# Three more ring slots from one large tile: storing the norm's input as four tiles, and tying the PSUM additions of a down projection behind a weight split

## The chip, the cores and the metric

The kernel runs on one core of a Trainium2 chip. The metric is the device time of one execution in microseconds. Before the change it is 2233.83 us, the median of three runs (2231.4, 2234.19 and 2233.83).

## What is computed

One layer of a streaming encoder for 256 tokens of width 2048, all in float32: a half-step SwiGLU FFN, two parallel token mixers (latent attention and RWKV7), cross-attention into 256 memory tokens, and a second half-step FFN. Only the two FFNs are touched by what follows, the down projection above all:

```
def rmsnorm(x, g): return x * rsqrt(mean(x * x, -1) + 1e-6) * g
def swiglu(h, w_gate, w_up, w_down):
    return (silu(h @ w_gate) * (h @ w_up)) @ w_down       # 256x2048 -> 256x5504 -> 256x2048

x = x + 0.5 * rmsnorm(swiglu(rmsnorm(x, n_ffn1_pre), ...), n_ffn1_post)
x = x + rmsnorm(mixers(rmsnorm(x, n_mix_pre)), n_mix_post)
x = x + rmsnorm(cross_attention(rmsnorm(x, n_x_pre), mem), n_x_post)
x = x + 0.5 * rmsnorm(swiglu(rmsnorm(x, n_ffn2_pre), ...), n_ffn2_post)
```

## The kernel before

**A weight tile's way.** Every weight is read once. A tile of 128 x 1024 float32 (512 KB) is loaded by SP's DMA queue into one of the four buffers `wraw` (L335, in the wide part L525). ScalarE casts it to the matmul's 32-bit type (`whi`, L343, L510) and VectorE subtracts the cast from the raw tile (`wlo`, L344, L511); the text calls the two a split, and `last_cast` and `last_split` name the latest ones. Both go to a slot of a ring: `RING` = 3 slots of `whi` and `wlo`. TensorE then does three products for each (activation high with weight high, high with low, low with high: L438 to L440, in the wide part L518 to L520), each with 512 columns.

**Order on the engines.** Each engine takes its instructions in the order of its own list, and so does SP, whose list is mostly loads: an instruction that waits holds all behind it. A scheduler makes these lists from the program and from priorities (`ahead(n)` moves a step n places forward); `after(a, b)` ties instruction a behind b. In the down projections TensorE's order is as written.

**The down projection.** 5504 rows are 43 blocks of 128, the 2048 columns two halves (b = 0 and 1) of 1024, each of them two chunks of 512 (c = 0, 1 and c = 2, 3). For a half the order is:

1. `lin_wide` (L496): the first 30 blocks over all 1024 columns. 16 blocks are single tiles of 12 matmuls. The other 14 go in 7 pairs, for which a scheme of Strassen's kind saves an eighth: a pair loads two tiles, splits half of one and the whole other, then VectorE makes four sums in place in the raw tiles (L543 to L546) and both are split again, for 21 matmuls. So a half has 30 loads, 44 splits and 339 matmuls. These splits go to a ring of six slots: the three of `whi` and `wlo`, then three in `room`, a 32 KB-per-partition tile that takes the place of `hT` (the norm's output, the FFN's input). Each half starts at slot 0.
2. `narrow`: early tiles e0 to e2 of the odd chunk (blocks 30 to 35 of c + 1, 128 x 1024 each: two blocks of 512 columns), in the ring of three.
3. `fix_wide` (L558): the pairs left four shared partial sums p1, p5, p7, p6 in PSUM. One ScalarE copy (L566) and eight VectorE additions and subtractions (L567 to L574) add them to the half's own four banks. A `wraw` buffer, `part`, holds the intermediate values. They have the priority `ahead(3 * self.lead)`.
4. `narrow`: n0 to n6, the last 13 blocks of the even chunk (n6 is one block, 128 x 512), after which the chunk is done: ScalarE squares and sums it (L617) and VectorE scales it by the gain (L758).
5. `narrow`: f0 to f3, the last 7 blocks of the odd chunk. In the first FFN's b = 1, f0 and f1 are split into slots of a `Passage`, which sit in the next norm's `hT`.

Then the residual X (2 MB) is loaded by four SP loads of 512 KB (L877), tied behind the latest split; the first FFN's X comes from the input x, the second's from `xsp`, where the running sum was stored. In the first FFN the next projection's weights (`w_in`) follow on SP, in the second X stands ahead of the very last weight tile.

Of the kernel before, what the change touches and what calls it, by code (L numbers as in the profile page):

```python
# [108 lines left out]

class Passage:  # L110
# [3 lines left out]
    def __init__(self, L, gain, spill=None, keep=None):  # L114
        self.L, self.gain, self.spill = L, gain, spill if keep is None else keep
        self.wide = spill is not None
        self.h = L.hpool.tile([P, KD, 2, T], F32R, tag="hT", name="hT", bufs=1)
        flat = self.h.rearrange("p k a t -> p (k a t)")
        at = lambda i: flat[:, KD * T + i * WT : KD * T + (i + 1) * WT]
# [84 lines left out]
class Layer:  # L204
# [291 lines left out]
    def lin_wide(self, w, b, mh, ml, sums, ring, banks):  # L496
# [25 lines left out]
        def load():  # L522
            raw = self.wraw.tile([P, WT], F32, tag="wraw", name="wraw")
# [7 lines left out]
        for item in _wide_order():  # L531
# [24 lines left out]
            product(own[1][0], at(k1, 1), e4)  # L556

    def fix_wide(self, banks, part):  # L558


        nc = self.nc
        own, (p1, p5, p7, p6) = banks
        u, v = part[:, :512], part[:, 512:]
        add, sub = nc.vector.tensor_add, nc.vector.tensor_sub
        with self.ahead(3 * self.lead):
            nc.scalar.copy(out=u, in_=p1)  # L566
            add(own[0][0], own[0][0], u)  # L567
            add(u, p6, u)
            sub(v, p5, u)
            add(u, p7, u)  # L570
            add(own[1][0], own[1][0], u)
            add(own[0][1], own[0][1], v)
            sub(v, v, p7)
            add(own[1][1], own[1][1], v)  # L574
# [71 lines left out]
    def pre_norm(self, gain, update):  # L646

        nc = self.nc
        h = self.hpool.tile([P, KD, 2, T], F32R, tag="hT", name="hT", bufs=1)
# [19 lines left out]
    def pre_norm_input(self, srcT, gain, pool, squares, order=False):  # L669
# [4 lines left out]
        h = pool.tile([P, KD, 2, T], F32R, tag="hT", name="hT", bufs=1)  # L674
# [95 lines left out]
    def ffn(self, normed, wg, wu, wd, post, residual, *after):  # L770
# [3 lines left out]
        with self.tc.tile_pool(name="hid", bufs=1) as hid:  # L774
# [32 lines left out]
            for c0 in range(0, DFF, 256):  # L807
# [38 lines left out]
            room = self.hpool.tile([P, KD * 2 * T], F32R, tag="hT", name="room", bufs=1)  # L846
            slots = [(x[:, a : a + WT], z[:, d : d + WT]) for x, z, d0 in (
                (self.whi, self.wlo, 0), (room, room, RING * SLOT)) for a in range(0, RING * SLOT, SLOT) for d in (a + d0,)]
            banks = {}

            def narrow(c, ks, ev, *args):
                base = c // 2 * KF * P * WT + (WIDE * WT + c % 2 * (KF - WIDE) * 512) * P
                self.lin_tok(
                    wd, KF, 0, 512, mh, ml, ev, *args, 0, [banks[c // 2][0][t][c % 2] for t in range(NT)],
                    (ks, lambda k: base + (k - WIDE) * P * 512))

            def lin(c, ev, passage):
# [9 lines left out]
                with self.tc.manual_schedule(engines={mybir.EngineType.PE}):  # L867
                    self.lin_wide(wd, b, mh, ml, lambda n: [(x[:, 0], x[:, 1]) for x in (sums(n)[:, i] for i in range(3))],
# [1036 lines left out]
```

## Time and profile before

The page is of one profiled execution; `PE` is TensorE's matmuls, `DVE` VectorE, `ACT` ScalarE, `SP` the queue that issues the loads.

| | us |
|---|---|
| median of three runs | 2233.83 |
| the profiled execution | 2234.2 |
| its span | 2232.4 |
| mean granted TensorE clock | 0.994 of full |
| VectorE busy | 1621.1 (73%) |
| ScalarE busy | 1190.6 (53%) |
| DMA | 453.51 MB, mean 203 GB/s |

The first FFN's down projection runs from 461 to 686 us, the second's from 1999 to 2219 us; the rest of the program isn't touched in TensorE's order. In a row of the timeline the bracket at the end is the idle time ahead of the instruction and what ended it.

### The profile page before, as it was taken

What the parts mean: (1) busy time and instruction counts of PE and PEld (TensorE: products, weight loads), DVE (VectorE), ACT (ScalarE), POOL (GpSimd) and SP (SyncE); (2) the same over time, 40 slices, a digit from 0 to 9 for tenths busy, and PEclk for the clock granted to TensorE, in tenths of its full rate; (3) what the DMA queues carried; (4) which work ended last, traced back from release to release, by engine and by line L of the source; (5) the groups of instructions that cost most, each with busy time, mean ns of one, the idle gap of its engine ahead of it and who ended that gap; (6) DMA issues with size and microseconds to landing.
All of it is one profiled execution on the core that took longest, in us unless ns stands there. A gap on an engine that the chain in (4) does not pass through costs nothing.

```text
span 2232.4 us, 35351 instructions
## 1 busy us (share of the span) xinstructions
PE 2176.8 (98%) x13580; PEld 1929.9 (86%) x13580; DVE 1621.1 (73%) x2402; ACT 1190.6 (53%) x1794; POOL 106.2 (5%) x177
## 2 busy tenths in 40 slices
PE   9999999999999999999999999999999999999997
PEld 8999999987878889988777889988999999988786
DVE  7777666687787667777777766557777766678685
ACT  7555555554545655664444556446555555555453
POOL 0000000000000100101342000000000000000000
PEclk9999999999999999999999999999999999999998
DMA  7666666655657664555867765556666666666655
GB/s 250 203 200 203 202 199 202 202 191 188 206 188 264 204 219 146 185 177 180 254 197 242 271 210 189 175 174 218 198 200 202 201 200 201 203 197 203 204 199 178
DMA packets 132361, 453.51 MB, mean 203 GB/s; under 512 B 16352, under 2 KB 17888, under 8 KB 131936
## 3 DMA queue, kind: packets, MB, share of 16 engines
q1 hardware_dynamic: 124560, 434.03, 59.7%
q0 software_dynamic: 6768, 16.79, 2.5%
q8 instruction: 106, 1.74, 0.3%
q14 instruction: 63, 0.52, 0.1%
q10 hardware_dynamic: 864, 0.44, 0.1%
HBM read 438.61 MB, written 12.59 MB: 202 GB/s over the span
## 4 chain that ended last, share of the span: by engine, by line
PE 68%; DVE 11%; DMA 9%; issue 7%; ACT 4%; POOL 1%; SPq 0%; ACTq 0%; DVEq 0%; POOLq 0%
PE mm L399 30%; PE mm L403 15%; DMA wraw<-in_w_ffn_down 7%; PE mm L439 6%; PE mm L438 6%; PE mm L440 6%; DVE wlo L344 3%; DVE room L511 3%; ACT whi L343 2%; DVE wlo L511 1%; ACT room L510 1%; DVE wraw L545 1%; PE mm L519 1%; PE mm L520 1%; DMA squares<-in_xT 1%
## 5 line engine op out<-in xcount | busy, mean ns | idle before, releaser
L344 DVE TENSOR_TENSOR wlo<-wraw,whi 128x1024 fp32r<-128x1024 f32 (+3 forms) x672 | 807.1, 1203 | 433.1 <-ACT whi L343 424.6
L399 PE MATMUL mm<-hT,whi 128*128 128x512 f32 x3280 | 1077.0, 383 | 1.7 <-ACT whi L343 1.1
L343 ACT CAST whi<-wraw 128x1024 fp32r<-128x1024 f32 (+3 forms) x672 | 691.5, 1030 | 594.1 <-PE mm L440 240.6
L403 PE MATMUL mm<-hT,wlo 128*128 128x256 f32 x3280 | 879.4, 273 | 0.8 <-DVE wlo L344 0.8
L399 PEld LDWEIGHTS mm<-hT,whi 128*128 128x128 f32 x3280 | 613.2, 189 | 82.9 <-ACT whi L343 2.6
L403 PEld LDWEIGHTS mm<-hT,wlo 128*128 128x128 f32 x3280 | 628.9, 192 | 7.4 <-DVE wlo L344 1.9
L439 PE MATMUL mm<-wlo,hT 128*128 128x512 f32 (+2 forms) x512 | 180.3, 352 | 4.1 <-DVE wlo L344 3.8
L438 PE MATMUL mm<-whi,hT 128*128 128x512 f32 (+2 forms) x512 | 182.5, 357 | 0.9 <-DVE gt L1564 0.7
L440 PE MATMUL mm<-whi,hT 128*128 128x512 f32 (+2 forms) x512 | 178.3, 349 | 0.1
L411 ACT COPY half<-mm 128x256 f32<-128x256 f32 x206 | 75.8, 369 | 116.2 <-PE mm L399 116.2
L510 ACT CAST whi<-wraw 128x1024 fp32r<-128x1024 f32 x92 | 94.2, 1046 | 66.0 <-DVE wraw L546 38.5
L511 DVE TENSOR_TENSOR wlo<-wraw,whi 128x1024 fp32r<-128x1024 f32 x92 | 110.4, 1222 | 16.9 <-ACT whi L510 16.1
L510 ACT CAST room<-wraw 128x1024 fp32r<-128x1024 f32 (+1 forms) x84 | 74.0, 903 | 84.9 <-DMA wraw<-in_w_ffn_down 71.9
L412 DVE TENSOR_TENSOR half<-half,mm 128x256 f32<-128x256 f32 x206 | 86.1, 418 | 39.9 <-ACT half L411 39.8
L439 PEld LDWEIGHTS mm<-wlo,hT 128*128 128x128 f32 x512 | 97.1, 190 | 19.1 <-DVE wlo L344 10.5
L518 PE MATMUL mm<-whi,mh 128*128 128x512 f32 x284 | 109.1, 384 | 4.5 <-ACT whi L510 4.5
L519 PE MATMUL mm<-wlo,mh 128*128 128x512 f32 x284 | 109.3, 385 | 1.6 <-DVE wlo L511 1.6
L520 PE MATMUL mm<-whi,ml 128*128 128x512 f32 x284 | 108.9, 383 | 0.0
L438 PEld LDWEIGHTS mm<-whi,hT 128*128 128x128 f32 x512 | 97.1, 190 | 12.6 <-DVE gt L1564 1.1
L440 PEld LDWEIGHTS mm<-whi,hT 128*128 128x128 f32 x512 | 97.1, 190 | 9.7 <-DVE hT L626 1.0
L511 DVE TENSOR_TENSOR room<-wraw,room 128x1024 fp32r<-128x1024 f32 (+1 forms) x84 | 86.1, 1045 | 17.1 <-ACT room L510 16.5
L590 POOL TENSOR_TENSOR rstd<-rstd,mhalf 128x1 f32<-128x1 f32 x22 | 15.4, 705 | 1724.3 <-DVE rstd L588 1724.3
(361 smaller groups left out, 2752.3 us busy)
## 6 DMA issues: line engine op xcount, KB each, us to landing
wraw<-in_w_ffn_up SPq DMA_DIRECT2D x171, 512.0 KB, 4.2
wraw<-in_w_ffn_gate SPq DMA_DIRECT2D x170, 512.0 KB, 4.2
wraw<-in_w_ffn_down SPq DMA_DIRECT2D x168, 512.0 KB, 4.4
wraw<-in_w_in SPq DMA_DIRECT2D x124, 512.0 KB, 4.0
wraw<-in_w_o SPq DMA_DIRECT2D x32, 512.0 KB, 4.2
wraw<-in_w_ckv SPq DMA_DIRECT2D x32, 512.0 KB, 3.6
wraw<-in_w_oa SPq DMA_DIRECT2D x16, 512.0 KB, 3.5
wraw<-in_w_ob SPq DMA_DIRECT2D x16, 512.0 KB, 4.6
```

The source lines that it names most:

```text
L343: cast = self.last_cast = nc.scalar.copy(out=hi[:, e], in_=raw[:, e])
L344: self.last_split = nc.vector.tensor_sub(out=lo[:, e], in0=raw[:, e], in1=hi[:, e].bitcast(F32))
L399: both = lambda: nc.tensor.matmul(ps[j], hi[:, s], self.woven(x[:, k]), start=(k == 0), stop=(k == nk - 1))
L403: nc.tensor.matmul(ps[j][:, 0, :], lo[:, s], self.woven(x[:, k, 0]), start=False, stop=False)
L438: nc.tensor.matmul(ps[t], part(xh, t, k), hi, start=(k == first and not begun), stop=False, **more)
L439: nc.tensor.matmul(ps[t], part(xh, t, k), lo, start=False, stop=False, **more)
L440: self.last_mm = nc.tensor.matmul(ps[t], part(xl, t, k), hi, start=False, stop=(k == last), **more)
L510: self.last_cast = nc.scalar.copy(out=hi, in_=raw)
L511: self.last_split = nc.vector.tensor_sub(out=lo, in0=raw, in1=hi.bitcast(F32))
L518: nc.tensor.matmul(bank, xh, hi, start=start, stop=False)
L519: nc.tensor.matmul(bank, xh, lo, start=False, stop=False)
L520: nc.tensor.matmul(bank, xl, hi, start=False, stop=stop)
```

## The change

- `hT`, the `Passage`'s copy of it, and `mT` are each four tiles of 8 KB per partition instead of one of 32 KB (`Quarters` passes indices on to them). In a down projection three of the four are `room` slots, each with high and low part, and the fourth, `raws`, is two more raw buffers: of six loads in `lin_wide` four go to `wraw` and two to `raws`.
- The wide ring begins at the narrow ring's next slot (`self.turn`) instead of slot 0, and `self.turn` moves on by the wide part's 44 splits.
- `fix_wide` loses its priority; its copy is tied behind the cast, and its first addition behind the split, of the latest tile written ahead of it (e2).
- In b = 1, X's loads no longer follow all tiles: `narrow` steps issue them at blocks 30, 33, 36 and 39 of c = 2, each tied behind the latest split. A step of `lin_tok_steps` comes once for each of the two token blocks, so each X load is issued twice.

```diff
+def quarters(pool, name="hT"):
+    return Quarters([pool.tile([P, 4, 2, T], F32R, tag="hT", name=name, bufs=4) for _ in range(4)])
...
-        self.h = L.hpool.tile([P, KD, 2, T], F32R, tag="hT", name="hT", bufs=1)
+        self.h = quarters(L.hpool)
...
         def load():
-            raw = self.wraw.tile([P, WT], F32, tag="wraw", name="wraw")
+            i = self.wide_at % 6
+            raw = raws[:, i - 4] if i > 3 else self.wraw.tile([P, WT], F32, tag="wraw", name="wraw")
...
+        self.cuts = turn[0]
...
-        with self.ahead(3 * self.lead):
-            nc.scalar.copy(out=u, in_=p1)
-            add(own[0][0], own[0][0], u)
...
+        self.after(nc.scalar.copy(out=u, in_=p1), self.last_cast)
+        self.after(add(own[0][0], own[0][0], u), self.last_split)
...
-            room = self.hpool.tile([P, KD * 2 * T], F32R, tag="hT", name="room", bufs=1)
...
+            room = [self.hpool.tile([P, 2, WT], F32R, tag="hT", name="room", bufs=4) for _ in range(RING)]
+            raws = self.hpool.tile([P, 2, WT], F32, tag="hT", name="raws", bufs=4)
...
+            def refill(k):
+                i = (k - WIDE) // 3
+                if "X" in fresh and i < 4:
+                    t, s = i // 2, slice(i % 2 * 1024, (i % 2 + 1) * 1024)
+                    self.after(nc.sync.dma_start(
+                        out=fresh["X"][:, t, s], in_=residual[t * P : (t + 1) * P, s]), self.last_split)
...
+                for k in self.lin_tok_steps(
...
+                    if c == 2 and k % 3 == WIDE % 3:
+                        refill(k)
...
+                    order = slots[self.turn :] + slots[: self.turn]
                     self.lin_wide(wd, b, mh, ml, lambda n: [(x[:, 0], x[:, 1]) for x in (sums(n)[:, i] for i in range(3))],
-                                  slots, banks[b])
+                                  order + more, raws, banks[b])
+                    self.turn = (self.turn + self.cuts % (2 * RING)) % RING if self.cuts % (2 * RING) < RING else self.turn
                     narrow(c + 1, range(WIDE, EARLY, 2), None, 0, None)
                     self.fix_wide(banks[b], self.wraw.tile([P, WT], F32, tag="wraw", name="part"))
+                    if b:
+                        self.X = fresh["X"] = self.hpool.tile([P, NT, D], F32, tag="big", bufs=1, name="X")
                     narrow(c, range(WIDE, KF, 2), ev, 0, None)
-                if b:
-                    self.X = self.hpool.tile([P, NT, D], F32, tag="big", bufs=1, name="X")
...
```

TensorE's and GpSimd's orders stay as they were. SP, in the first FFN's b = 1, before: the tail of the wide loads, the first row of which is L525, then the narrow tiles (L335), X (L877) and the next projection.

```order
L525 DMA wraw<-in_w_ffn_down 128x1024 x21
L335 DMA wraw<-in_w_ffn_down 128x1024 x9
L335 DMA wraw<-in_w_ffn_down 128x512
L335 DMA wraw<-in_w_ffn_down 128x1024 x3
L335 DMA wraw<-in_w_ffn_down 128x512
L877 DMA X<-in_x 128x1024 x4
L335 DMA wraw<-in_w_in 128x1024 x4
```

SP at the same place after: L357 is the narrow tiles' load (the first six of them e0 to n2), L879 the X load.

```order
L357 DMA wraw<-in_w_ffn_down 128x1024 x6
L879 DMA X<-in_x 128x1024 x2
L357 DMA wraw<-in_w_ffn_down 128x1024
L879 DMA X<-in_x 128x1024 x2
L357 DMA wraw<-in_w_ffn_down 128x1024
L879 DMA X<-in_x 128x1024
L357 DMA wraw<-in_w_ffn_down 128x1024
L357 DMA wraw<-in_w_ffn_down 128x512
L879 DMA X<-in_x 128x1024 x2
L357 DMA wraw<-in_w_ffn_down 128x1024 x2
L879 DMA X<-in_x 128x1024
L357 DMA wraw<-in_w_ffn_down 128x1024
```

Eight X loads now stand among the narrow tiles n2 to f2, where four stood behind f3. The first two X loads and the fifth are first loads, tied behind the splits of n0, n1 and n3; the third, fourth and sixth write the same bytes again, each behind the landing of the load that it repeats; the seventh is the fourth quarter (behind n4's split) and the eighth its repeat. The second FFN has the same pattern, with `xsp` for `in_x`.

VectorE at `fix_wide` of b = 1 in the first FFN, before: L344 is the split of a narrow tile, the first of them e0's, and L567 to L574 are the additions.

```order
L344 TENSOR_TENSOR wlo<-wraw,whi 128x1024
L567 TENSOR_TENSOR mm<-mm,part 128x512
L344 TENSOR_TENSOR wlo<-wraw,whi 128x1024
L568 TENSOR_TENSOR part<-mm,part 128x512
L569 TENSOR_TENSOR part<-mm,part 128x512
L344 TENSOR_TENSOR wlo<-wraw,whi 128x1024
L570 TENSOR_TENSOR part<-mm,part 128x512
L571 TENSOR_TENSOR mm<-mm,part 128x512
L344 TENSOR_TENSOR wlo<-wraw,whi 128x1024 x2
L572 TENSOR_TENSOR mm<-mm,part 128x512
```

After: L366 is the narrow split, and L590 to L597 are the additions.

```order
L366 TENSOR_TENSOR wlo<-wraw,whi 128x1024 x3
L590 TENSOR_TENSOR mm<-mm,part 128x512
L591 TENSOR_TENSOR part<-mm,part 128x512
L592 TENSOR_TENSOR part<-mm,part 128x512
L593 TENSOR_TENSOR part<-mm,part 128x512
L594 TENSOR_TENSOR mm<-mm,part 128x512
L366 TENSOR_TENSOR wlo<-wraw,whi 128x1024 x2
L595 TENSOR_TENSOR mm<-mm,part 128x512
L596 TENSOR_TENSOR part<-part,mm 128x512
L366 TENSOR_TENSOR wlo<-wraw,whi 128x1024
L597 TENSOR_TENSOR mm<-mm,part 128x512
```

The splits of e0 to e2 moved ahead of all additions; the next two (n0, n1) stand behind five of them.

VectorE a little later, at the end of n6 in the second FFN's b = 1, before: the first row holds splits n2 to n5, then come n6's (512 columns), f0's and f1's; L758 is the chunk's scaling by the gain.

```order
L344 TENSOR_TENSOR wlo<-wraw,whi 128x1024 x4
L344 TENSOR_TENSOR wlo<-wraw,whi 128x512
L344 TENSOR_TENSOR wlo<-wraw,whi 128x1024 x2
L758 TENSOR_TENSOR y<-mm,g 128x512
L344 TENSOR_TENSOR wlo<-wraw,whi 128x1024
L758 TENSOR_TENSOR y<-mm,g 128x512
```

After: n3 to n5, n6, the scaling (L781) of the first token block, two small steps of its sum of squares, and only then f0.

```order
L366 TENSOR_TENSOR wlo<-wraw,whi 128x1024 x3
L366 TENSOR_TENSOR wlo<-wraw,whi 128x512
L781 TENSOR_TENSOR y<-mm,g 128x512
L608 TENSOR_REDUCE tot<-ss 128x1
L609 TENSOR_SCALAR tot<-tot 128x1
L366 TENSOR_TENSOR wlo<-wraw,whi 128x1024
L781 TENSOR_TENSOR y<-mm,g 128x512
```

The splits of f0 and f1 moved behind the scaling. On ScalarE the casts moved in the same way: f0's now stands behind the first square (L640, L617 before), where f0's and f1's stood ahead of it. In the first FFN it is the same in b = 1, where f0 to f3 stood ahead.

More of the change, by code (lines that the diff above doesn't have):

```diff
@@ L845, in ffn @@
                 self.lin_ch(wu, KD, c0, n, h, ev_up)
[L846 to L848 removed]
+            room = [self.hpool.tile([P, 2, WT], F32R, tag="hT", name="room", bufs=4) for _ in range(RING)]
+            raws = self.hpool.tile([P, 2, WT], F32, tag="hT", name="raws", bufs=4)
+            slots = [(self.whi[:, a : a + WT], self.wlo[:, a : a + WT]) for a in range(0, RING * SLOT, SLOT)]
+            more = [(x[:, 0], x[:, 1]) for x in room]
+            fresh = {}
+            def refill(k):
[4 more added lines that the diff above has]
+                        out=fresh["X"][:, t, s], in_=residual[t * P : (t + 1) * P, s]), self.last_split)
             banks = {}
```

48 lines of the change are left out of this document (28 added, 20 removed).

## The prediction

> **What bounds the kernel now.** I read the page's busy times first, then TensorE's waits, then a table of stretches over the two down projections, then timelines around the stalls.
>
> ```profile
> PE 2176.8 (98%) x13580; PEld 1929.9 (86%) x13580; DVE 1621.1 (73%) x2402; ACT 1190.6 (53%) x1794; POOL 106.2 (5%) x177
> PE mm L439 <- DVE wlo L344: 11.2, 13, 2.3
> PE mm L519 <- DVE wlo L511: 9.1, 18, 1.0
> PE mm L518 <- ACT whi L510: 5.0, 4, 3.4
> ```
>
> TensorE is the bound: busy for 2176.8 of 2232.4 us, and its order doesn't change. So the change can only remove, or add, waits of TensorE. L518 and L519 are the wide part, L439 mostly the narrow tiles. The stretches (columns: length, then busy time and count of PE, PEld, DVE, ACT, POOL, then clock, DMA share and GB/s; for each half the wide part, then the narrow tiles):
>
> ```profile
> 461.20:541.10 79.90, 76.42 (x339) 64.87 (x339) 68.03 (x76) 42.25 (x47) 0.00 (x0) 0.98 0.56 189
> 541.10:575.00 33.90, 31.56 (x137) 27.11 (x138) 19.27 (x22) 11.65 (x16) 0.00 (x0) 0.95 0.56 180
> 575.00:657.00 82.00, 78.91 (x358) 66.73 (x357) 67.57 (x74) 43.60 (x50) 0.00 (x0) 1.00 0.63 205
> 657.00:694.00 37.00, 34.35 (x151) 29.05 (x149) 23.87 (x31) 15.72 (x21) 0.55 (x1) 0.95 0.71 234
> 1987.00:2064.00 77.00, 73.97 (x337) 62.66 (x336) 67.04 (x76) 42.67 (x47) 0.00 (x0) 1.00 0.61 200
> 2064.00:2098.70 34.70, 34.70 (x162) 30.38 (x162) 21.60 (x24) 14.52 (x18) 0.00 (x0) 1.00 0.67 212
> 2098.70:2180.00 81.30, 76.20 (x341) 64.97 (x340) 68.55 (x75) 42.95 (x50) 0.00 (x0) 0.98 0.57 194
> 2180.00:2221.00 41.00, 36.78 (x155) 30.66 (x155) 21.41 (x28) 13.94 (x19) 0.45 (x1) 0.92 0.55 179
> ```
>
> A matmul that isn't held up starts 0.216 us after the one before (the first two rows below: 539.47 and 539.68). So a stretch loses its length less 0.216 times its count: 79.90 - 339 x 0.216 = 6.7 us, then 4.3, 4.7, 4.4, 4.2, -0.3, 7.6 and 7.5. That is 39 us, and with 1.2 us just ahead of the first stretch (below) **40 us** are there to be won. TensorE at the first half's `fix_wide`, at two starts of a wide part, and VectorE beside the first:
>
> ```profile
> 539.47 0.38 PE L519 MATMUL mm<-wlo,mh 128*128 128x512 f32 x1
> 539.68 0.38 PE L520 MATMUL mm<-whi,ml 128*128 128x512 f32 x1
> 541.19 0.48 PE L438 MATMUL mm<-whi,mh 128*128 128x512 f32 x1 [1.13 <-ACT whi L343]
> 543.92 0.48 PE L439 MATMUL mm<-wlo,mh 128*128 128x512 f32 x1 [2.24 <-DVE wlo L344]
> 544.53 0.63 PE L438 MATMUL mm<-whi,mh 128*128 128x512 f32 x1
> 544.96 0.63 PE L439 MATMUL mm<-wlo,mh 128*128 128x512 f32 x1
> ...
> 461.24 0.48 PE L518 MATMUL mm<-whi,mh 128*128 128x512 f32 x1 [1.18 <-ACT whi L510]
> 462.50 0.80 PE L519 MATMUL mm<-wlo,mh 128*128 128x512 f32 x1 [0.78 <-DVE wlo L511]
> ...
> 2102.51 0.48 PE L518 MATMUL mm<-whi,mh 128*128 128x512 f32 x1 [3.35 <-ACT whi L510]
> ```
>
> ```profile
> 537.75 1.23 DVE L344 TENSOR_TENSOR wlo<-wraw,whi 128x1024 fp32r<-128x1024 f32 x1 [1.68 <-ACT whi L343]
> 538.89 0.69 DVE L567 TENSOR_TENSOR mm<-mm,part 128x512 f32<-128x512 f32 x1
> 541.32 0.68 DVE L568 TENSOR_TENSOR part<-mm,part 128x512 f32<-128x512 f32 x1
> 542.65 1.22 DVE L344 TENSOR_TENSOR wlo<-wraw,whi 128x1024 fp32r<-128x1024 f32 x1
> ```
>
> After a stall matmuls start 0.43 us apart (544.53, 544.96) at half rate, for about nine: 9 x 0.21 = 1.9 us on top of the wait.
>
> **The change part by part.**
>
> *Ring order.* A wide part starts with slot 0 whichever slot the narrow tiles used last, so its first cast can wait for a slot that TensorE has only just left: the two starts above cost 1.18 + 0.78 + 1.9 = 3.9 us and 3.35 + 1.9 = 5.3 us, 9.2 together. With the oldest slot first the cast comes two tiles earlier, 24 matmuls or 5.2 us, more than either wait. I take 8.2 and leave 1.
>
> *Six raw buffers.* SP's wide loads wait for VectorE to give a raw buffer back, and VectorE and ScalarE in turn for landings (views of the waits in the first FFN):
>
> ```profile
> SPq L525 <- DVE wraw L545: 53.0, 9, 6.8
> DVE wraw L544 <- DMA wraw<-in_w_ffn_down: 6.9, 10, 1.0
> ACT room L510 <- DMA wraw<-in_w_ffn_down: 38.4, 26, 3.3
> ```
>
> The steady loss of the wide parts is what the starts leave: 6.7 + 1.2 - 3.9 = 4.0, then 4.7, 4.2 and 7.6 - 5.3 = 2.3: 15 us. VectorE is busy for some 68 us of a half whose 339 matmuls need 73.2, so it can keep up, with 5 us to spare, if it needn't wait for landings. Two more buffers let SP issue two loads earlier; a half's 30 loads take 73.2 us, so two are 4.9 us, more than the longest of these waits (3.3). With so thin a margin I take 11 and leave 4; ends: 0 (VectorE is the bound) and 15.
>
> *`fix_wide`'s tie.* Before, additions of 0.69 us stand among the splits of e0 to e2, and these splits release TensorE (row 543.92). The narrow stretches lose 4.3, 4.4, -0.3 and 7.5 us, of which about 1 is the last tile (below). With all three splits ahead, e0 to e2 give TensorE 36 x 0.216 = 7.8 us; five additions take 3.5 us and n0's split 1.2, so they lie beside that work, if e2's split ends by 3 us into it. I take 14.5 and leave 0.5. If that cover is gone, 2 us per half come back.
>
> *X's place.* Before, X stood ahead of the last tile of the second FFN; about 1 us of waiting ahead of that tile goes (counted above). Removed in all: 8.2 + 11 + 14.5 + 1 = **35 us**.
>
> *What X adds.* Every X load is issued twice, the repeat waits for the first's landing, and SP holds the weight tiles behind it. Landings of narrow weight tiles (541 to 564 us), of X in the first FFN, and in the second:
>
> ```profile
> DMA to landing us min/median/max: 3.4/4.2/5.4
> ...
> DMA to landing us min/median/max: 6.4/7.6/8.7
> ...
> DMA to landing us min/median/max: 7.3/8.6/9.7
> ```
>
> Call the landing time L. The second X load goes out at n1's split, its repeat and then n4's load at L after it, and n4 is there after 2L. A narrow tile is 12 x 0.216 = 2.59 us of TensorE. n1's cast waits for the end of e1, three tiles before in the ring; cast (1.05) and split (1.23) end 2.3 us later. n4's cast can start at the end of n1, 7.8 us after that of e1, and may come 2.9 us later still before TensorE waits. So n4 costs 2L - 8.4: nothing at 4.2, 1.6 at 5, 6.8 at 7.6. The same reckoning for f2 (the last repeat goes ahead of it, at n4's split) gives 2L - 13: nothing up to 6.5. Between n2 and f2 some 4 MB of weights and 4 MB of X pass in 26 us, 310 GB/s where the narrow stretch had 234 at a share of 0.71. So L is above 4.2; the 7.6 and 8.6 were of four loads issued at once. I take 5, nearest to the unhurried row.
>
> The Trainium skill ("DMA: Bandwidth & Descriptors", Anatomy of one DMA) fits a transfer as 2.0 us plus bytes over 436 GB/s, for GpSimd's path. By it 512 KB land in an estimated 3.2 us, n4 costs nothing and the sum is 3.2 us less; the row has 4.2 here and no such landing under 3.4.
>
> *f0 behind the square.* In b = 1 the cast of f0 now waits for the chunk's first square, thus for nearly the end of n6. The second FFN's end, ScalarE then VectorE:
>
> ```profile
> 2211.27 0.59 ACT L617 ACTIVATE junk<-mm 128x512 f32<-128x512 f32 x1
> 2211.85 1.03 ACT L343 CAST whi<-wraw 128x1024 fp32r<-128x1024 f32 x1
> 2217.28 0.62 ACT L343 CAST whi<-wraw 128x512 fp32r<-128x512 f32 x1 [3.80 <-DMA wraw<-in_w_ffn_down]
> ...
> 2212.54 0.68 DVE L758 TENSOR_TENSOR y<-mm,g 128x512 f32<-128x512 f32 x1
> 2213.14 1.22 DVE L344 TENSOR_TENSOR wlo<-wraw,whi 128x1024 fp32r<-128x1024 f32 x1
> ```
>
> The square begins at the end of the first token block's products, three matmuls (0.65 us) before n6 ends. Square, cast and split, 0.59 + 1.03 + 1.22 = 2.84, less 0.65 and the one matmul that needs no split (0.22), leave 2.0; with handovers 2.4. It is split in two like the pair of waits at 461.24 (1.18 and 0.78), after which matmuls ran at half rate: 1.9 more. The ends are 2.0 and 4.3.
>
> The Trainium skill ("TensorE: Matmul & The Clock Gate", What's actually happening) has TensorE go to half rate after an idle window of some 3.4 us. By it the new stalls stay at full rate and the sum is 2 x 1.9 = 3.8 us less. Here the rows at 461 speak against it, with two waits of 1.96 us in all.
>
> Added: 1.6 + 2.4 + 1.9 = 5.9 per FFN, **12 us** in both. The profiled execution took 2234.2, its span 2232.4, and lies 0.4 above the median: 2234.2 - 35 + 12 = **2211 us**.
>
> **The rivals.**
>
> *All is hidden.* L stays at 4.2, the stalls of f0 stay at full rate, the wide parts lose nothing: 2234.2 - 40 + 2 x 2.4 = 2199. For it: the unhurried row. Against: 310 GB/s. Chance 0.14.
>
> *VectorE is the bound of the wide parts.* The raw buffers then bring nothing: 2211 + 11 = 2222. For it: 68 of 73.2 us busy, in which every handover counts. Against: the rows that end in a landing. Chance 0.14.
>
> *The repeats hold SP's queue.* At the 9.2 us to which the X rows reach, n4 costs 10.0, f2 5.4, f0 with half rate 4.3 and a second half-rate stretch 1.9: 21.6 per FFN, 43 in both, and 2234.2 - 35 + 43 = 2242, slower. It decides from 2L - 8.4 + 2L - 13 + 6.2 = 17.5 per FFN, which is L = 8.2. For it: X's own rows of 7.6 and 8.6. Against: these were four at once with 2 MB of weights behind. Chance 0.06; L within 0.2 of 8.2 leaves the time as it was.
>
> *The change doesn't reach TensorE*, because what SP waits for in the wide part isn't buffers but VectorE's own pace, and the new stalls eat the rest. With L near 7.6 and the raw buffers idle, 35 - 11 = 24 us go and 2 x (6.8 + 2.2 + 6.2) = 30 come: 2240, slower too; with L at 6.5 it is 2 x (4.6 + 6.2) = 22 and about 2232. Chance 0.05 for no change, 0.02 for slower.
>
> **How the numbers follow.** Some 0.2% (4.5 us) is what a measurement tells from no change. My case, 2205 to 2219, has 0.59; hidden 0.14 and VectorE-bound 0.14 are faster too: 0.87. No change has 0.05, slower 0.08. The range reaches from the hidden case, 2198, to L = 7 in my case (5.6 + 1 + 6.2 = 12.8 per FFN, 2234.2 - 35 + 26 = 2225); above it lie the 0.13 of the last two rivals, and some 0.05 of tails lie outside on either side.
>
> **What would show it.** In the profile after: at the four starts of the wide parts no wait of L518 above 0.5 us; VectorE's waits on landings in the wide parts gone, TensorE at 73 to 74.5 us for 339 matmuls; no wait between e0 and n1; in each b = 1 a wait for f0's cast and split of 2 to 2.5 us, matmuls 0.43 us apart after it, and n4 late by 1 to 2. I am wrong if X lands in 7 us or more, if the wide parts still take over 76 us, or if SP's repeats cost nothing.

## The result and the profile after

The changed kernel takes 2213.14 us (median of four runs, 2210.27 to 2216.57), the kernel before 2233.84 beside it: a ratio of 0.991, 95% interval 0.9893 to 0.9927, thus 20.7 us faster. The forecast was 2211, range 2198 to 2225. The profiled execution of the changed kernel is the slowest of the four (2216.57, span 2214.7), so its profile shows 17.6 us less than the profile before.

The first row is TensorE's of the page; then come the eight stretches, cut this time at the first matmul of each wide part and of each e0 (columns as before):

```profile
PE 2170.6 (98%) x13580; PEld 1929.0 (87%) x13580; DVE 1618.7 (73%) x2402; ACT 1189.7 (54%) x1794; POOL 106.0 (5%) x177
```

```profile
460.77:537.82 77.05, 75.39 (x341) 65.17 (x339) 68.53 (x77) 43.70 (x48) 0.00 (x0) 0.98 0.63 221
537.82:571.49 33.67, 33.67 (x158) 29.48 (x156) 20.82 (x24) 15.25 (x19) 0.00 (x0) 1.00 0.67 212
571.49:644.66 73.17, 73.17 (x341) 64.07 (x340) 67.14 (x74) 41.70 (x47) 0.00 (x0) 1.00 0.62 205
644.66:690.06 45.40, 37.82 (x158) 29.73 (x157) 24.52 (x32) 16.46 (x23) 0.55 (x1) 0.96 0.76 263
1979.97:2053.60 73.63, 73.49 (x340) 63.91 (x339) 68.25 (x77) 42.99 (x48) 0.00 (x0) 1.00 0.67 230
2053.60:2087.27 33.67, 33.67 (x157) 29.48 (x156) 20.82 (x24) 15.26 (x19) 0.00 (x0) 1.00 0.67 210
2087.27:2160.44 73.17, 73.17 (x341) 64.07 (x339) 67.12 (x74) 41.46 (x47) 0.00 (x0) 1.00 0.62 206
2160.44:2203.86 43.42, 37.43 (x157) 29.95 (x155) 21.36 (x29) 13.73 (x19) 0.55 (x1) 0.96 0.61 206
```

A wide part of 339 matmuls needs 73.2 us at 0.216 each, a narrow stretch of 156 needs 33.7. Four of the eight stretches now lose nothing, the two wide parts among them with VectorE still busy for 67 of 73.17 us, and a fifth loses 0.4. What is left sits in the first wide part (3.8 us) and in the two narrow stretches in which X is loaded: 45.40 - 33.7 = 11.7 and, up to the very last matmul, 43.42 - 33.5 = 9.9.

TensorE's order is the same in every kernel of this study, so its waits can be compared matmul by matmul. This table is worked out from the matmul starts in each trace: time from the last matmul ahead of a stretch to the last in it, less 0.216 us for each matmul ("1" and "2" are the two FFNs, "w" the wide and "n" the narrow stretch of half b; "median" is of the kernel's own runs under that name):

```
kernel                1 w0  1 n0  1 w1  1 n1  2 w0  2 n0  2 w1  2 n1   sum   median us
before                 6.8   5.6   5.2   4.3   4.7   0.0   8.0   7.8  42.4   2233.8
changed                3.8   0.0  -0.1  11.7   0.4   0.0  -0.1   9.9  25.7   2213.1
x_once                 0.5   0.0  -0.1   2.4   0.4   0.0  -0.1   2.8   5.9   2196.6
x_tiny                 1.3   0.0  -0.1   4.4   0.5   0.0  -0.1   3.5   9.5   2199.3
x_aside                2.2   0.0  -0.1  10.9   0.4   0.0   0.3  12.5  26.1   2213.7
x_aside_spread         0.4   0.0   0.4   8.8   0.5   0.0   0.7   7.6  18.3   2210.8
x_late                 0.4   0.0  -0.1  -0.3   0.8   0.0   0.0   1.0   1.8   2195.7
late_fix_ahead         1.6   0.0   0.3  -0.3  -0.1   0.0   0.5   1.0   2.8   2193.4
late_slot0             9.5   3.0  -0.1  -0.2   3.0   0.0   7.1   3.9  26.2   2217.8
x_once_4raw            4.4   0.0   6.1   2.4   3.4   0.0   7.8   6.0  30.1   2219.1
ring_only              4.6   0.0   5.8  -0.3   4.2   0.0   7.9   1.2  23.4   2213.5
raws_only              8.4   2.6  -0.1  -0.2   4.4   0.0   5.9   4.2  25.2   2215.8
```

With X's cost set apart (the two n1 columns against those of x_late: 12.0 + 8.9 = 20.9), the change removed 42.4 - (25.7 - 20.9) = 37.6 us of waiting and added 20.9. Here is where the 20.9 come from, SP and then ScalarE in the first FFN's b = 1, and the landings of X there and of the narrow tiles issued from 650 to 664 us:

```profile
651.83 1.46 SPq L879 DMA_DIRECT2D X<-in_x  x2
653.38 0.38 SPq L357 DMA_DIRECT2D wraw<-in_w_ffn_down  x1
655.10 4.42 SPq L879 DMA_DIRECT2D X<-in_x  x2
659.61 0.38 SPq L357 DMA_DIRECT2D wraw<-in_w_ffn_down  x1
663.01 0.33 SPq L879 DMA_DIRECT2D X<-in_x  x1
663.44 0.88 SPq L357 DMA_DIRECT2D wraw<-in_w_ffn_down  x2
```

```profile
660.68 1.04 ACT L365 CAST whi<-wraw 128x1024 fp32r<-128x1024 f32 x1 [7.00 <-DMA wraw<-in_w_ffn_down]
666.31 1.05 ACT L365 CAST whi<-wraw 128x1024 fp32r<-128x1024 f32 x1 [4.59 <-DMA wraw<-in_w_ffn_down]
```

```profile
DMA to landing us min/median/max: 3.2/5.7/6.7
...
DMA to landing us min/median/max: 6.5/6.6/7.2
```

n3 goes out at 653.38 behind two X loads and n4 at 659.61 behind two repeats; ScalarE's casts of them wait at 660.68 for 7.00 us and at 666.31 for 4.59 us, each for a landing. Weight tiles that took 4.2 us in the kernel before take 6.6 here. Tile by tile, by the same count, the first and the second FFN lose 4.4 and 4.1 us at n3, 1.4 and 1.2 at n4, 1.1 and 1.8 at n5, and 4.8 and 2.9 from f0 on.

### The profile page after: what moved, and what is told of

It reads as the page before. It is cut to its first block, busy times and chain, and to the rows that moved or that the text cites. A ratio compares the mean times of both kernels' runs of the same rounds, so it can differ in the third digit from the quotient of the medians.

```text
span 2214.7 us, 35352 instructions
## 1 busy us (share of the span) xinstructions
PE 2170.6 (98%) x13580; PEld 1929.0 (87%) x13580; DVE 1618.7 (73%) x2402; ACT 1189.7 (54%) x1794; POOL 106.0 (5%) x177
## 4 chain that ended last, share of the span: by engine, by line
PE 80%; issue 7%; DMA 4%; DVE 4%; ACT 2%; POOL 1%; SPq 0%; DVEq 0%; POOLq 0%; ACTq 0%
PE mm L421 31%; PE mm L425 15%; PE mm L460 6%; PE mm L461 6%; PE mm L462 6%; PE mm L541 4%; PE mm L542 4%; PE mm L540 4%; DVE wlo L366 2%; ACT whi L365 1%; DMA wraw<-in_w_ffn_down 1%; DMA raws<-in_w_ffn_down 1%; DMA X<-xsp 0%; DMA X<-in_x 0%; DMA ab<-vsh 0%
## 5 line engine op out<-in xcount | busy, mean ns | idle before, releaser
L366 DVE TENSOR_TENSOR wlo<-wraw,whi 128x1024 fp32r<-128x1024 f32 (+3 forms) x672 | 806.4, 1203 | 434.9 <-ACT whi L365 426.4
L541 PE MATMUL mm<-wlo,mh 128*128 128x512 f32 x284 | 108.4, 382 | 1.1 <-DVE wlo L533 1.0
L540 PE MATMUL mm<-whi,mh 128*128 128x512 f32 x284 | 108.5, 382 | 0.7 <-ACT whi L532 0.7
L461 PE MATMUL mm<-wlo,mh 128*128 128x512 f32 x200 | 78.2, 391 | 6.5 <-DVE wlo L366 6.5
L532 ACT CAST room<-wraw 128x1024 fp32r<-128x1024 f32 (+1 forms) x56 | 49.7, 893 | 63.3 <-DVE wraw L567 53.2
L460 PE MATMUL mm<-whi,mh 128*128 128x512 f32 x200 | 77.5, 388 | 5.1 <-ACT whi L365 5.1
L533 DVE TENSOR_TENSOR wlo<-wraw,whi 128x1024 fp32r<-128x1024 f32 x60 | 71.8, 1222 | 14.5 <-ACT whi L532 13.7
```

Source lines behind the costliest of these rows:

```text
L366: self.last_split = nc.vector.tensor_sub(out=lo[:, e], in0=raw[:, e], in1=hi[:, e].bitcast(F32))
L460: nc.tensor.matmul(ps[t], part(xh, t, k), hi, start=(k == first and not begun), stop=False, **more)
L461: nc.tensor.matmul(ps[t], part(xh, t, k), lo, start=False, stop=False, **more)
L540: nc.tensor.matmul(bank, xh, hi, start=start, stop=False)
L541: nc.tensor.matmul(bank, xh, lo, start=False, stop=False)
```

## The experiments

The runs below come from three more chips; each ratio is to the kernel before on the same chip (2232.03, 2230.06 or 2231.02 us). The theory on the loss was the prediction's: repeats of X loads hold SP's queue while they wait. Its rivals were the doubled bytes, and X's early place as such.

### X once, and the waits and the bytes apart

`x_once` issues each X quarter at its first turn only:

```diff
-                if "X" in fresh and i < 4:
-                    t, s = i // 2, slice(i % 2 * 1024, (i % 2 + 1) * 1024)
+                if "X" in fresh and i < 4 and i not in fresh:
+                    t, s = fresh[i] = i // 2, slice(i % 2 * 1024, (i % 2 + 1) * 1024)
```

> The changed kernel (2213.1 us) with each X quarter loaded once, so no load waits for the landing of another. Matmul by matmul, the profile of the changed kernel gains some 38 us on the one before in the wide parts and around the additions in PSUM, and gives 11.4 and 9.2 us back in the two stretches in which X is loaded. Theory 1, the repeats hold SP's queue with their waits and thereby make the weight tiles behind them late: almost all of the 20 us come back, 2194 to 2198, and no weight tile of the last narrow stretch is waited for over 1 us. Theory 2, the doubled bytes slow all landings: half of them are gone, and half of the loss, 2202 to 2206. Theory 3, X's place among the narrow tiles costs by itself: 2208 to 2213.

2196.58 us (2194.87 to 2203.76), ratio 0.9853 (0.983 to 0.9877). Nearly all of the loss came back; X's early place costs at most little. SP and ScalarE at the same place:

```profile
647.69 1.46 SPq L879 DMA_DIRECT2D X<-in_x  x2
649.24 3.11 SPq L357 DMA_DIRECT2D wraw<-in_w_ffn_down  x4
657.92 0.33 SPq L879 DMA_DIRECT2D X<-in_x  x1
```

```profile
655.59 1.05 ACT L365 CAST whi<-wraw 128x1024 fp32r<-128x1024 f32 x1 [6.06 <-DMA wraw<-in_w_ffn_down]
656.85 1.04 ACT L365 CAST whi<-wraw 128x1024 fp32r<-128x1024 f32 x1 [0.22 <-DMA wraw<-in_w_ffn_down]
```

n3 to n6 go out in one row. n3 is still late, behind two X loads, and TensorE loses 1.8 us there in the first FFN and 2.8 in the second; n4 is there almost at once. The narrow tiles issued from 646 to 660 us don't land sooner than in the changed kernel, though no X load is repeated:

```profile
DMA to landing us min/median/max: 5.2/6.7/7.0
```

So a landing of 6.7 us alone does little harm: n4 to n6 are issued early enough for it. With the repeats gone the scheduler also puts the casts of f0 and f1 ahead of the square again, by itself: that order was a consequence of the repeats.

`x_tiny` keeps the repeat and its wait, but only 16 of its 1024 columns:

```diff
-                    t, s = i // 2, slice(i % 2 * 1024, (i % 2 + 1) * 1024)
+                    t, s = i // 2, slice(i % 2 * 1024, i % 2 * 1024 + fresh.get(i, 1024)); fresh[i] = 16
```

> The changed kernel with the repeat of each X load cut from 1024 columns to 16: the repeat still waits for the landing of the first load and holds SP's queue, but its bytes are gone. Theory 1, the waits: most of the loss stays, 2205 to 2211 (a little less than in the changed kernel, since landings are shorter). Theory 2, the bytes: like the kernel with single loads, which it puts at 2202 to 2206, with the weight tiles landing in under 5 us and no stall. If theory 1 is right for the single loads and the wait costs nothing once the bytes are gone, it comes out with them, at 2194 to 2198.

2199.34 us (2198.59 to 2203.01), ratio 0.9863 (0.9844 to 0.9882): 2.8 us above x_once by the medians, with intervals that overlap. SP still waits, and narrow tiles issued from 646 to 660 us land sooner:

```profile
650.47 0.38 SPq L357 DMA_DIRECT2D wraw<-in_w_ffn_down  x1
652.08 3.92 SPq L879 DMA_DIRECT2D X<-in_x  x2
656.10 0.85 SPq L357 DMA_DIRECT2D wraw<-in_w_ffn_down  x2
```

```profile
DMA to landing us min/median/max: 3.5/4.3/6.5
```

n4 goes out at 656.10, 5.6 us behind n3, and is still there in time. In all, SP's waits for landings of X from 640 to 680 us come to 10.3 us here, against 13.0 in the changed kernel. So theory 1 in its plain form fell: the waits alone cost little. Of the order behind the square a part is here too: f0's cast stands ahead of the chunk's first square again, f1's stays behind it. TensorE loses 2.5 us at f1 in the first FFN (1.09 + 1.04 + 0.33), where that cast also waits 1.04 us for its landing, and about 1 in the second.

`x_aside` keeps the bytes and takes the waits away: a repeat goes to a tile that nobody reads.

```diff
+                    to = fresh["X"][:, t, s]
+                    if i in fresh:
+                        if i % 2 == 0:
+                            fresh["aside"] = self.hpool.tile([P, 2, WT], F32, tag="hT", name="aside", bufs=4)
+                        to = fresh["aside"][:, i % 2]
+                    fresh[i] = True
-                        out=fresh["X"][:, t, s], in_=residual[t * P : (t + 1) * P, s]), self.last_split)
+                    self.after(nc.sync.dma_start(out=to, in_=residual[t * P : (t + 1) * P, s]), self.last_split)
```

> The changed kernel with every X quarter still loaded twice, but the second time into a tile that nobody reads (two tiles of 8 KB in the place of the room slots, free by then), so that no load waits for the landing of another: the doubled bytes without the waits. With single loads 2196.6, with waits but 16-column repeats 2199.3, with both 2213.1. If the waits make the loss but only through landings that the bytes lengthen (each wait then lasts 6 us instead of 3 to 4): 2198 to 2203, of which some 3 us are the casts of f0, which stand behind the chunk's square here too. If the bytes alone make it: 2208 to 2213. Halves: 2204 to 2207.

2213.7 us (2211.9 to 2215.05), ratio 0.992 (0.9899 to 0.9941): the whole loss without SP waiting for a landing once. SP, and the landings of the four tiles in its last row here:

```profile
649.26 0.33 SPq L885 DMA_DIRECT2D X<-in_x  x1
649.64 0.42 SPq L885 DMA_DIRECT2D aside<-in_x  x1
650.40 0.33 SPq L885 DMA_DIRECT2D X<-in_x  x1
650.77 0.43 SPq L885 DMA_DIRECT2D aside<-in_x  x1
651.30 2.91 SPq L357 DMA_DIRECT2D wraw<-in_w_ffn_down  x4
```

```profile
DMA to landing us min/median/max: 8.7/9.5/9.6
```

n3 to n6 are issued together at once, but behind 2 MB, and land after 9.5 us. That burst doesn't stand so in the changed kernel, so `x_aside_spread`, with x_once's single loads, puts the second loads about where the changed kernel's repeats stand: two behind n3, two among f0 to f2, each tied to a split that is done by then (a function called beside `refill` at blocks 34, 40 and 42 instead of the lines above):

```diff
+            def aside(k):
+                for i in {34: (0, 1), 40: (2,), 42: (3,)}.get(k, ()) if "X" in fresh and k not in fresh else ():
...
+                    self.after(nc.sync.dma_start(
+                        out=fresh["aside"][:, i % 2], in_=residual[t * P : (t + 1) * P, s]), self.last_split)
```

> As x_aside (every X quarter loaded twice, the second time into a tile that nobody reads, no load waits for the landing of another), but the second loads stand on SP's queue where they stand in the changed kernel: two behind n3, two among f0 to f2, each tied to a split that is done by then, so that SP doesn't hold for it. x_aside put 2 MB ahead of n3 in one burst, which could be its own loss. If the bytes by themselves lengthen landings enough to stall TensorE wherever they stand: 2208 to 2213, with n3 and n4 waited for. If what counts is what stands ahead of a needed tile at the moment it is issued, the burst in x_aside and the landing wait in the changed kernel: 2198 to 2204, of which some 3 us are the casts of f0 behind the square.

2210.76 us (2207.7 to 2212.61), ratio 0.9906 (0.9893 to 0.992). The expectation that only the burst did it is wrong. But it isn't a clean proof for the bytes either:

```profile
653.38 0.41 SPq L357 DMA_DIRECT2D wraw<-in_w_ffn_down  x1
658.63 0.33 SPq L879 DMA_DIRECT2D X<-in_x  x1
659.06 1.33 SPq L357 DMA_DIRECT2D wraw<-in_w_ffn_down  x3
...
664.56 1.56 ACT L365 CAST whi<-wraw 128x1024 fp32r<-128x1024 f32 x2 [3.47 <-DMA wraw<-in_w_ffn_down]
```

Between n4 (653.38) and n5 (659.06) SP holds for the third X load, which is tied to n3's split, and n3 is late. So here another hold on the same queue, that of X's own tie, takes the place of the landing wait. What the four runs show together: beside x_once, x_tiny, which has SP's waits without the doubled bytes, loses 2.8 us; the three kernels with the doubled bytes (changed, x_aside, x_aside_spread) lose 14 to 17 us (medians, partly of different chips), whether SP waits for landings or not. But the bytes don't act by the landing time alone, which is as long in x_once. The changed kernel and x_aside_spread have both, tiles that SP issues late and landings of some 6 us and more; x_tiny has the late issue alone (landings of 4.3 us), x_once the long landings alone; and x_aside, with no late issue by a landing wait, has landings of 9.5 us. So the loss fits the sum of the hold and the landing, as the prediction's 2L has it. That the bytes would cost as much if SP held for nothing and no burst stood ahead of n3 was not tried.

### X in its old place

`x_late` issues the four loads once, behind the narrow steps, as before the change:

```diff
-                    if c == 2 and k % 3 == WIDE % 3:
-                        refill(k)
+                    pass
...
-                    if b:
-                        self.X = fresh["X"] = self.hpool.tile([P, NT, D], F32, tag="big", bufs=1, name="X")
                     narrow(c, range(WIDE, KF, 2), ev, 0, None)
+                if b:
+                    self.X = fresh["X"] = self.hpool.tile([P, NT, D], F32, tag="big", bufs=1, name="X")
+                    for k in range(WIDE, WIDE + 12, 3):
+                        refill(k)
```

> The changed kernel with X's four loads in their old place, behind the narrow tiles, once each. Theories 1 and 2: the 20 us come back but for the last tile of the second feed-forward part, which again stands behind X (it lost about 1 us before): 2194 to 2199. Theory 3, the early place costs by itself: the same here, and the kernel with single early loads is 10 us or more slower than this one. If both are within 2 us of each other, the early place is worth nothing.

2195.72 us (2195.25 to 2196.44), ratio 0.9844 (0.9826 to 0.9861), and on another chip:

> The kernel with X's single loads in their old place, again, beside the same kernel with the additions' old priority on the same chip. 2194 to 2197.

2195.97 us (2194.36 to 2198.6), ratio 0.9842 (0.9828 to 0.9855). Within 1 us of x_once: the early place wins nothing and costs nothing that can be measured in the whole. In the profiled executions it costs 4.1 us in the two down projections (5.9 against 1.8 in the table) and wins about as much behind the first of them: TensorE's first transposition there waits 2.78 us for VectorE's new X in x_late and not at all in x_once. The last tile still waits some 1 us behind X (column 2 n1).

### The raw buffers

`x_once_4raw` is x_once with all wide loads in the four old buffers:

```diff
-            raw = raws[:, i - 4] if i > 3 else self.wraw.tile([P, WT], F32, tag="wraw", name="wraw")
+            raw = self.wraw.tile([P, WT], F32, tag="wraw", name="wraw")
```

> The kernel with single X loads, but all loads of the wide part into the four old raw buffers, none into the two new ones. My prediction: the two buffers bring 11 us, so 2205 to 2209. Rival, VectorE sets the pace of the wide parts: 0 to 3 us, 2195 to 2200. A third possibility: they bring something in the steady state but cost it at the first feed-forward's start, where the first load into a new buffer landed 7.7 us after its issue and TensorE waited: then that stall (about 3 us with its half-rate matmuls) is gone here and the steady losses of 4 to 5 us per half are back.

2219.08 us (2214.62 to 2219.94), ratio 0.9942 (0.9924 to 0.996): 22.5 us slower than x_once, twice my term. Its first FFN's second wide part and its second FFN's, against 73.17 us each with six buffers:

```profile
571.46:650.80 79.34, 75.37 (x341) 63.53 (x340) 68.71 (x75) 42.41 (x48) 0.00 (x0) 1.00 0.62 201
2086.23:2167.28 81.05, 75.54 (x341) 63.59 (x339) 68.68 (x75) 42.47 (x48) 0.00 (x0) 1.00 0.58 197
```

These lose more than the kernel before did in the same place (6.1 and 7.8 against 5.2 and, after its start, some 1.7): with the oldest slot first and no second pair of buffers, the steady losses grow.

`raws_only` is the other way round, the kernel before with the four tiles and six buffers and nothing else (late_fix_ahead with late_slot0's edit).

> The kernel before the change (2233.8 us) with nothing but the four tiles and the two extra raw buffers: wide ring from slot 0, additions with their old priority, X in its old place, once. My prediction's term for the buffers: 11 us, 2221 to 2225. Rival, from the run with four buffers, which was 22.5 us slower than its partner: they are worth about 20 us by themselves, 2211 to 2216. Rival: the parts need each other, and alone the buffers bring under 5 us, 2229 to 2234.

2215.77 us (2212.93 to 2217.48), ratio 0.9929 (0.9904 to 0.9955): 14.3 us alone. The steady losses go, and so does more than half of the waits around the additions (the four narrow stretches lose 6.6 us in all, 17.7 before), while the waits at the starts grow (8.4 us in the first FFN's first wide part, 6.8 before).

### The ring order

`late_slot0` is x_late with this edit:

```diff
-                                  order + more, raws, banks[b])
-                    self.turn = (self.turn + self.cuts % (2 * RING)) % RING if self.cuts % (2 * RING) < RING else self.turn
+                                  slots + more, raws, banks[b])
```

> The kernel with X's single loads in their old place (2195.7 us), but every wide part starts at slot 0 as before the change. My prediction's term for the ring order: 8.2 us, 2202 to 2206, with the waits of L540 at the starts of the wide parts back (1 to 3.4 us and half-rate matmuls behind them). Rival: with two more raw buffers and the additions moved, slot 0 is free in time: 2195 to 2198.

2217.78 us (2216.75 to 2218.89), ratio 0.9939 (0.9919 to 0.9959): 22 us slower than x_late, where I had 8.2. The start of the first wide part, TensorE and then ScalarE:

```profile
465.56 0.80 PE L540 MATMUL mm<-whi,mh 128*128 128x512 f32 x1 [5.61 <-ACT whi L532]
...
463.51 1.04 ACT L532 CAST room<-raws 128x1024 fp32r<-128x1024 f32 x1 [1.83 <-DMA raws<-in_w_ffn_down]
464.46 1.04 ACT L532 CAST whi<-wraw 128x1024 fp32r<-128x1024 f32 x1
```

TensorE waits for the cast at 464.46. Since its slot comes free last, the scheduler has put that cast behind others, one of which waits for a load into `raws`. And 3.0 and 3.9 us are back in the narrow stretches, though the additions are tied as in the change. `raws_only` differs from `late_slot0` by the tie alone and was measured on the same chip: 2215.77 us without it, 2217.78 with it, with ranges that overlap.

`ring_only` is the kernel before with the four tiles and the ring order alone (late_fix_ahead with x_once_4raw's edit: four buffers, additions with their old priority, X late).

> The kernel before the change with the four tiles and the ring order alone: four raw buffers, additions with their old priority, X in its old place. My prediction's term: 8.2 us, so about 2222 to 2226 beside 2230 to 2234. From the run without it, which lost 22 us at the starts and around the additions: the starts (12.6 us before) and the waits around the additions (16.7 us) go almost wholly, the steady loss of the wide parts stays or grows to the 22 us of the run with four buffers: 2213 to 2219.

2213.5 us (2211.53 to 2214.8), ratio 0.9919 (0.9906 to 0.9933), 17.5 us alone. Its first two narrow stretches:

```profile
538.06:571.73 33.67, 33.67 (x158) 29.48 (x156) 20.27 (x24) 14.77 (x18) 0.00 (x0) 1.00 0.68 216
...
650.79:684.17 33.38, 33.38 (x157) 29.04 (x156) 21.60 (x30) 15.03 (x20) 0.55 (x1) 1.00 0.81 268
```

Not a matmul is late there, with the additions among the splits as before the change. So the interleaved additions by themselves make no wait at `fix_wide`; with the oldest slot first it is gone, and with two more raw buffers alone it shrinks.

### The tie of the additions

`late_fix_ahead` is x_late with `fix_wide` as it was before the change:

```diff
-        self.after(nc.scalar.copy(out=u, in_=p1), self.last_cast)
-        self.after(add(own[0][0], own[0][0], u), self.last_split)
+        with self.ahead(3 * self.lead):
+            nc.scalar.copy(out=u, in_=p1)
+            add(own[0][0], own[0][0], u)
...
```

> The kernel with X's single loads in their old place (2195.7 us), but the copy and additions of the shared sums with their old priority and no tie behind cast and split. My prediction's term: 14.5 us, 2207 to 2212, with the waits of 2.2 us for the split of e0 back in three of the four halves. Rival: the waits there came from the late loads of e0 to e2, which the extra buffers bring earlier, and not from the order of the additions: 2195 to 2199.

2193.44 us (2190.9 to 2194.51), ratio 0.9828 (0.9807 to 0.9849), on another chip than x_late. On one chip with it:

> The kernel with X's single loads in their old place and the additions' old priority, again, beside the same kernel with the tie on the same chip. If the tie is worth nothing, both agree within 2 us; if the tie costs, this one is 2 us or more faster; my prediction's term (14.5 us for the tie) would make it far slower and has already failed.

2193.81 us (2192.14 to 2194.23), ratio 0.983 (0.9817 to 0.9844), beside x_late's 2195.97. The tie is worth nothing; if anything it costs 2 us, though the intervals overlap. The two kernels differ most behind the first FFN's last narrow tile, where TensorE's first transposition waits 2.78 us for VectorE's new X with the tie (x_late) and 1.76 us without (late_fix_ahead_again); why was not followed further. `late_fix_ahead` is the fastest kernel of the study: 1.7% below the kernel before, 0.9% below the changed one.

## Why the prediction was right, and where it was not

**TensorE as the bound, and 40 us to be won: right.** 42.4 us by the matmul count, and x_late has 1.8 of them left.

**The sum of what goes, 35 us: about right (37.6), but its parts were not.** Of the three terms only the buffers' came near. Apart by place, from the same matmul starts:

```
kernel      first 24 matmuls of the wide parts   rest of the wide parts   narrow stretches
before                 10.5                              14.3                   17.7
raws_only              18.4                               0.2                    6.6
ring_only               0.0                              22.5                    0.9
x_late                  0.0                               1.2                    0.6
```

- *Six raw buffers, 11 us of the steady losses:* the mechanism was right: 14.1 of 14.3 us of steady loss go, and the wide parts run at 73.17 us with VectorE at 67, so VectorE as the bound (chance 0.14) is refuted. That they alone bring 14.3 us by the medians, near my term, is luck in part: in that trace 11.1 us around the additions go as well, which I had put down to the tie, and 7.9 us more are lost at the starts. Taken out of x_once, they cost 22.5 us.
- *Ring order, 8.2 us:* less than half of it, 17.5 alone and 22 when taken out of x_late. I priced only the waits at the starts; 16.8 us in the narrow stretches go as well, and with four raw buffers some 8 us of steady loss come in return.
- *`fix_wide`'s tie, 14.5 us:* this step failed; the tie brings nothing. I read the additions among the splits as the cause, since the split that released TensorE at 543.92 came behind them. But I took the splits for those of e0, e1, e2 in that order. The part on the change says so too of the first FFN's b = 1, where the first split is e2's and e0's comes second. In the program's own list, which has the tiles' numbers (SP loads e0 as 4886, then e1 as 4902, then e2 as 4918), VectorE's order before was, in the first half,

```
L344 TENSOR_TENSOR wlo_114<-wraw_4902,whi_112 128x1024
L567 TENSOR_TENSOR mm_4361<-mm_4361,part_4934 128x512
L344 TENSOR_TENSOR wlo_114<-wraw_4918,whi_112 128x1024
L568 TENSOR_TENSOR part_4934<-mm_4368,part_4934 128x512
L569 TENSOR_TENSOR part_4934<-mm_4366,part_4934 128x512
L344 TENSOR_TENSOR wlo_114<-wraw_4886,whi_112 128x1024
```

  e1, e2, and only then e0, which TensorE needs first. e0's slot was the one that the wide part had used last, so the scheduler let the others pass. The kernel before has the opposite case too: in the second FFN's first half, where nothing is lost (0.0 in the table), the additions stand among the splits in the same pattern, but e0 has the oldest slot and its split comes first. With the ring order alone the wait is gone; with the tie and six raw buffers but slot 0 (late_slot0) 3.0 and 3.9 us of it stay, in the two halves in which e0's split comes last. The tie with four buffers and slot 0 was not run. The same holds for the first cast of a wide part.

**X's loads, 12 us: the place was right, the size was not (20.9 in the profile, 16.6 by the medians of changed and x_once).** The term was n4's cost, 2L - 8.4 with L = 5, and L is what was mis-sized. Narrow tiles took 6.6 us to land there, for which the formula gives 4.8 instead of 1.6 per FFN; by the end of n4 the two FFNs had lost 5.8 and 5.3. With x_tiny's median of 4.3 it gives 0.2, and n4 was in time there. n4 itself was late by 1.4 and 1.2 us, within the 1 to 2 that I named, but only because TensorE already stood 4.4 and 4.1 behind at n3. Two things the term left out: n3 stands behind two X loads that are tied to splits, so it is late by itself (1.8 and 2.8 us in x_once, more with longer landings), and n5 to f1 stand behind further X loads. My reason against a long L, that the rows of 7.6 and 8.6 us were of four loads at once, was too weak: the tiles behind two X loads or two repeats took 6 to 7 us as well. And neither the wait alone (x_tiny) nor the long landing alone (x_once) is the loss; the two together are.

**f0 behind the square, 2.4 us and then 1.9 at half rate:** a wait came, near the size I gave, but only a part of it is the square's, and the half rate did not come. TensorE in the changed kernel at f0 of the first FFN, at n3, and at the first wide part:

```profile
677.38 0.48 PE L460 MATMUL mm<-hT,mh 128*128 128x512 f32 x1 [1.06 <-ACT hT L365]
678.64 0.48 PE L461 MATMUL mm<-hT,mh 128*128 128x512 f32 x1 [0.78 <-DVE hT L366]
678.96 0.38 PE L462 MATMUL mm<-hT,ml 128*128 128x512 f32 x1
679.18 0.38 PE L460 MATMUL mm<-hT,mh 128*128 128x512 f32 x1
...
661.78 0.48 PE L460 MATMUL mm<-whi,mh 128*128 128x512 f32 x1 [1.42 <-ACT whi L365]
663.04 0.73 PE L461 MATMUL mm<-wlo,mh 128*128 128x512 f32 x1 [0.78 <-DVE wlo L366]
663.56 0.63 PE L462 MATMUL mm<-whi,ml 128*128 128x512 f32 x1
663.99 0.63 PE L460 MATMUL mm<-whi,mh 128*128 128x512 f32 x1
...
466.81 0.48 PE L540 MATMUL mm<-whi,mh 128*128 128x512 f32 x1 [0.69 <-ACT whi L532]
468.26 0.51 PE L541 MATMUL mm<-wlo,mh 128*128 128x512 f32 x1 [0.96 <-DVE wlo L533]
468.58 0.62 PE L542 MATMUL mm<-whi,ml 128*128 128x512 f32 x1
468.99 0.63 PE L540 MATMUL mm<-whi,mh 128*128 128x512 f32 x1
```

Waits of 1.06 + 0.78 us at f0 were followed by full rate (0.22 from start to start), 1.42 + 0.78 at n3 and 0.69 + 0.96 at the start by half rate (0.43). At f0 the cast could have begun some 0.7 us earlier in its old order: its load went out at 669.58 behind X's and landed 6.0 us later, at 675.6, and the cast began at 676.29. In the second FFN the same reckoning gives 1.1 us.

**The start of the first wide part** kept 3.8 us in the profiled execution, but 0.4 and 0.5 in those of x_late and x_once, which start it in the same way. It sits at the third tile (the rows at 466.81 and 468.26), which has the slot that was used last; the cast for it stands behind another that waited 1.82 us for the first load into `raws`, 0.3 us in x_late. Such a wait, and the half rate behind it, may be what sets the slowest of the four runs apart; only that one has a profile.

So that 35 - 12 = 23 came near the 20.7 measured is in part luck: 14.5 us of the gain stood at a step that brings nothing and came from the ring and the buffers instead, and both sides were too small, by some 3 and 9 us.

## What to carry to other kernels

Where buffers are reused in a ring, look at whose turn the first tile after a change of phase falls on: a slot that was used last makes not only that tile late, but lets a scheduler put it behind others, and the stall then shows at whatever stands between. Read such lists with the tiles' numbers before naming a cause. And count how often a generator's step comes: the loads issued twice cost 16.6 us here, more than the waits of their repeats alone (2.8 us with 16 columns), since late issue and landings of 6 to 7 us add up for all that stands behind on the queue.

## What the runs showed of the hardware

- Half rate after a stall does not follow from the length of the wait: 1.65 us of waits (rows at 466.81 and 468.26) were followed by it, with a granted clock of 0.53 from 468.4 to 472 us; 1.84 us (677.38 and 678.64) were not (clock 1.00 from 678.9 to 681.3), nor were 2.28 us (1.50 + 0.78) at n3 of the second FFN in x_once (clock 1.00). The Trainium skill ("TensorE: Matmul & The Clock Gate", What's actually happening) ties the half rate to an idle window of some 3.4 us that runs on by itself. That a shorter wait has it and longer ones do not agrees with a free-running window; that 1.65 us with matmuls close by on both sides were enough does not agree with 3.4 us of idle time.
- The landing time of a 512 KB tile depends on what is under way when it is issued: 4.2 us in the kernel before, 4.3 with the small repeats, 6.6 with full repeats, 6.7 without repeats but with four tiles in a row behind two X loads (x_once), 9.5 behind a burst of 2 MB.
